# A 96-byte tile that nothing uses, opened first on the right side of SBUF

## The chip, the cores and the metric

The kernel runs as one program on one core of a Trainium2 chip. The core has five instruction streams that matter here: TensorE for matmuls (PE in the profile; its weight loads have a row of their own, PEld), VectorE (DVE), ScalarE (ACT), GpSimd (POOL) and SyncE (SP), which in this kernel issues every DMA. The metric is the device time of one execution in microseconds, taken as the median of several executions.

## The reference, cut to what matters

One layer of a hybrid streaming encoder in float32, for a prompt of 2048 tokens and a sample of 32 tokens with a cache of 128.

```python
qa, ka, va, qb, kb, vb = split_proj(rmsnorm(hp, g_attn[i]), w_in[i])   # 1024 -> 3072 columns
oa = diff_attn_prompt(qa, ka, va, t5_table, lam)     # group A: 4 heads, two score maps each, all earlier chunks
ob = band_attn_prompt(qb, kb, vb, band_table[i])     # group B: 8 heads, this chunk and the 8 before it
hp = hp + merge(oa, ob, subln_g[i], out_norm_b[i], w_out[i], lam_init)
c  = rmsnorm(h, g_mlp)
h  = h + jnp.square(jax.nn.relu(c @ w_up)) @ w_down                    # 1024 -> 4096 -> 1024
return h + jax.nn.sigmoid(h @ w_ple_gate) * (p @ w_ple_proj)
```

A last rmsnorm gives the outputs; the keys and values are outputs too. The sample goes through the same layer with its cache.

## The kernel before, in words

**Numbers as pairs.** A float32 product is made from two rounded parts. `split` writes the rounded part of a tile (`hi`, on ScalarE) and the rest (`lo`, a subtraction on GpSimd or VectorE). `mm3` then multiplies hi by hi, hi by lo and lo by hi (lines 216, 217 and 218) and adds the three in PSUM. In `mm3` the left member of a term is the stationary operand, which a weight load puts into the array, and the right member is the moving operand, which is read from SBUF column by column while the next weight load runs. In the profile a matmul is named out<-moving,stationary. In the products with weights the weight is stationary and the activation moves, except in the value projection `vps`, where the weight moves.

**Stages.** The 2080 tokens are four blocks, 512, 512, 512 and 544. Through the first 2050 us or so come the projections (`qps`, `vps`), both attentions (`s`, `sb`, `tpp`, `tpb`, `o`, `ob`), the output projection (`ops`) and the MLP of blocks 0 and 1 (`mlp`, with `ups` and `dps`). Then the gate of block 1 (`gps`, `pps`), the output projection of blocks 2 and 3, the gate of block 0, the MLP of block 2 (`mlp7`), the gate of block 2, the MLP of block 3 and its gate. `mlp7` makes the up projection with seven products of half size in place of eight, so its `ups` matmuls move 256 columns for block 2 and 272 for block 3, from the operand tiles `cs`. Its `dps` matmuls move the activations `uh` and `ul`, 512 columns for block 2 and twice 272 for block 3.

**Two sides of SBUF.** Each partition of SBUF is handed out from both ends. A pool opened with `side="left"` (the default) lies above the pools opened before it on the left; one with `side="right"` lies below those opened before it on the right. A tile takes a multiple of 32 bytes in each partition. A pool's place is thus the sum of the sizes of the pools that are open before it on its side. In the compiled program of the kernel before, the right side begins at byte 229,344, which is 32 past a multiple of 64. Where the right-side pools then lie:

| pool | opened for | tiles, bytes each | lowest byte | over a multiple of 64 |
|---|---|---|---|---|
| `pp0` | first blocks' inputs `x`, `xt` | 6 of 4096, 9 of 32 | 204,480 | 0 |
| `wv0` | first value weights `wh0`, `wl0` | 8 of 4096 | 171,712 | 0 |
| `a0`, `a1`, `b`, `wq` | attention, norms | `ka`, `e`, `pH`, `v`, `q` and others | 129,248 (`a1`) | 32 |
| `uh` | activations: `ou`, `hu`, `uh`, `ul`, `pT` | 20 of 2176 | 185,824 | 32 |
| `wx` | the fourth of each ring of weight pieces, `s2` | 5 of 2048 | 175,584 | 32 |
| `wk4` | temporaries and raw weights of the last stages | 2176 and 4096 | 136,928 | 32 |
| `fk4` | last norm: `gf` and small tiles | one of 4096, 21 pieces of 32 | 132,160 | 0 |
| `cs` | operands of `mlp7`; last gate's `hc` | 14 of 4352 | 71,232 | 0 |

The tiles of the left side that take part in matmuls (`aH`, `wh`, `wl`, `cH`, `hH`, the left pieces, and `uh` of the earlier MLP in pool `uq`) lie at multiples of 64. Columns within these tiles are taken in steps of 1024, 1088, 2048 or 2176 bytes, all multiples of 64, so a slice keeps its tile's remainder.

**Weights of the last stages.** From about 2120 us on `wunit` cuts each weight unit into two halves, and each half takes a hi and a lo piece from two rings whose turns go three times to the left (pool `wp4`) and once to the right (pool `wx`): `self.pieces = [Rings(*[(self.wp, t)] * 3, (wx, t)) for t in ("wh", "wl")]`. Every fourth piece is on the right.

**Order of the work.** Each engine runs one stream of instructions in an order fixed when the program is built, by a planner that sorts the work by priorities and by its own estimate of times. Buffers are handed out in rings: a tile waits for the last reader of the buffer that it takes over, also where the bytes belonged to a closed pool.

Of the kernel before, what the change touches and what calls it, by code (L numbers as in the profile page):

```python
# [13 lines left out]
F32 = mybir.dt.float32  # L14
# [6 lines left out]
P = 128  # L21
# [122 lines left out]
class Kern:  # L144
# [1311 lines left out]
    def run(self):  # L1456
        tc, nc, a = self.tc, self.nc, self.a
        with ExitStack() as top:

            def opened(stack, name, bufs, space=None, side="left"):  # L1460
                kw = {} if space is None else {"space": space}
                return stack.enter_context(
                    tc.tile_pool(name=name, bufs=bufs, side=side, reuse_waits="tile", **kw)
                )
# [4 lines left out]
            wpx = ExitStack()  # L1469
            self.wp = opened(wpx, "wp", 3)  # L1470
            self.rawp = Rings((self.wp, "wr"))
            mm = opened(top, "mm", MM, PSUM)
            tp = mm
            psx = ExitStack()
# [237 lines left out]
```

## Time and profile before

| | us |
|---|---|
| median of 3 runs | 3154.2 |
| lowest, highest | 3153.26, 3156.3 |
| profiled execution, its span from first to last instruction | 3144.6 |
| TensorE busy in the span | 3011.4 |
| VectorE, ScalarE, GpSimd busy | 1897.6, 1878.1, 1847.6 |

Of the profiled execution the page gives the span alone; the median of the runs is 9.6 us above it, which is the time around the span. The span is one execution's. A row of the page names a line, an engine, an operation and the tiles, and then tells the count, the time in sum and the mean of one in ns; a matmul's duration there is longer than the distance to the next one's start, since matmuls overlap. The timeline gives starts, and from a row of matmuls without a gap the time that one takes from the stream is (last start - first start) / count.

### The profile page before, as it was taken

Reading aid. Unit: us, or ns where it says so; the run is one execution under the profiler, and the core shown is the slowest. Engines: PE = TensorE matmul, PEld = TensorE weight load, DVE = VectorE, ACT = ScalarE, POOL = GpSimd, SP = SyncE. Lnnn points to the kernel's source line nnn. Section 1 sums busy time; section 2 is a strip of 40 time slices with the busy share of each in tenths; the row PEclk is TensorE's granted clock in tenths of the full one; section 3 lists DMA queues with packets and bytes.
Section 4 is the critical chain, followed back from the end, with each engine's and each line's share of the span. In section 5 each row is a group of like instructions: output and inputs, shape, how many; then the busy total and the mean of one; then the engine's idle time right before and its main releaser. Section 6 shows DMA issues by size and latency. Waiting matters only on the chain. (4 is left out here: it accounts for less than half of the span.)

```text
span 3144.6 us, 52811 instructions
## 1 busy us (share of the span) xinstructions
PE 3011.4 (96%) x17913; PEld 2649.6 (84%) x17913; DVE 1897.6 (60%) x4596; ACT 1878.1 (60%) x4166; POOL 1847.6 (59%) x2496
## 2 busy tenths in 40 slices
PE   8999898999999999999999999999899999999998
PEld 7787786899977887878788888878788887999998
DVE  5157774645465654666756556535667885576653
ACT  6257775766676764776666656554555455554545
POOL 2357455332345644665655545667877888667674
PEclk9999999999999999999999999999999999999999
DMA  8788757986788746555564543437533446333231
GB/s 281 244 244 244 204 185 229 263 232 201 205 250 230 218 130 153 152 154 153 157 184 130 144 123 103 145 116 241 179 128 115 144 152 229 123 107 107 88 116 56
DMA packets 523287, 539.27 MB, mean 171 GB/s; under 512 B 38749, under 2 KB 401569, under 8 KB 523017
## 3 DMA queue, kind: packets, MB, share of 16 engines
q1 hardware_dynamic: 523016, 535.89, 57.5%
q8 instruction: 142, 2.33, 0.3%
q14 instruction: 129, 1.05, 0.1%
HBM read 421.97 MB, written 117.75 MB: 172 GB/s over the span
## 5 line engine op out<-in xcount | busy, mean ns | idle before, releaser
L176 POOL TENSOR_TENSOR wl<-wr,wh 128x256 fp32r<-128x256 f32 x648 | 475.6, 766 | 354.8 <-ACT wh L181 315.7
L181 ACT ACTIVATE piece<-wr 128x512 fp32r<-128x512 f32 x406 | 246.1, 626 | 272.7 <-PE ups L217 113.1
L176 POOL TENSOR_TENSOR piece<-wr,piece 128x256 fp32r<-128x256 f32 x404 | 327.4, 837 | 99.7 <-ACT piece L181 86.4
L181 ACT ACTIVATE wh<-wr 128x1024 fp32r<-128x1024 f32 x228 | 241.2, 1058 | 171.7 <-PE qps L217 40.7
L166 POOL TENSOR_TENSOR wl<-wr,wh 128x256 fp32r<-128x256 f32 x264 | 199.4, 787 | 194.1 <-ACT wh L181 183.9
L216 PE MATMUL dps<-uh,piece 128*128 128x272 f32 (+1 forms) x768 | 247.0, 325 | 7.5 <-ACT piece L181 3.2
L166 POOL TENSOR_TENSOR piece<-wr,piece 128x256 fp32r<-128x256 f32 x280 | 237.0, 878 | 26.9 <-ACT piece L181 21.5
L218 PE MATMUL dps<-uh,piece 128*128 128x272 f32 (+1 forms) x768 | 247.8, 325 | 1.6 <-POOL piece L166 1.3
L217 PE MATMUL dps<-ul,piece 128*128 128x272 f32 (+1 forms) x768 | 247.8, 323 | 0.0
L216 PE MATMUL ups<-cs,piece 128*128 128x256 f32 (+1 forms) x864 | 246.0, 285 | 1.0 <-DVE r L1232 1.0
L217 PE MATMUL ups<-cs,piece 128*128 128x256 f32 (+1 forms) x864 | 245.3, 284 | 0.0
L218 PE MATMUL ups<-cs,piece 128*128 128x256 f32 (+1 forms) x864 | 245.2, 284 | 0.0
L216 PE MATMUL qps<-aH,wh 128*128 128x512 f32 (+1 forms) x640 | 231.2, 361 | 7.3 <-ACT kn L506 4.0
L218 PE MATMUL qps<-aH,wl 128*128 128x512 f32 (+1 forms) x640 | 229.5, 359 | 0.0
L217 PE MATMUL qps<-aL,wh 128*128 128x512 f32 (+1 forms) x640 | 228.5, 357 | 0.0
L1173 DVE TENSOR_TENSOR h<-h,dps 128x512 f32<-128x512 f32 x256 | 174.3, 683 | 80.9 <-PE dps L218 75.4
L1221 DVE TENSOR_TENSOR h<-h,dps 128x272 f32<-128x272 f32 (+1 forms) x384 | 189.3, 515 | 51.8 <-PE dps L218 50.8
L216 PE MATMUL dps<-uh,wh 128*128 128x512 f32 x512 | 207.8, 406 | 9.4 <-DVE h L1173 5.7
L216 PE MATMUL ups<-cH,wh 128*128 128x512 f32 x512 | 202.8, 396 | 2.1 <-ACT cH L181 1.1
L638 PE MATMUL s<-ka,q 128*128 128x512 f32 (+3 forms) x768 | 187.2, 345 | 15.9 <-ACT e L652 7.1
L218 PE MATMUL dps<-uh,wl 128*128 128x512 f32 x512 | 201.7, 394 | 0.5 <-POOL wl L166 0.4
L217 PE MATMUL ups<-cL,wh 128*128 128x512 f32 x512 | 201.2, 393 | 0.0
(317 smaller groups left out, 9634.2 us busy)
## 6 DMA issues: line engine op xcount, KB each, us to landing
wr<-w_up SPq DMA_DIRECT2D x128, 512.0 KB, 4.0
wr<-w_down SPq DMA_DIRECT2D x128, 512.0 KB, 3.8
wr<-w_in SPq DMA_DIRECT2D x74, 512.0 KB, 5.1
q<-qS SPq DMA_DIRECT2D x128, 256.0 KB, 5.4
v<-vSa SPq DMA_DIRECT2D x64, 512.0 KB, 3.9
ka<-kS SPq DMA_DIRECT2D x32, 512.0 KB, 8.9
wr<-w_out SPq DMA_DIRECT2D x32, 512.0 KB, 4.7
wr<-w_ple_gate SPq DMA_DIRECT2D x32, 512.0 KB, 4.3
```

Of the source, the lines that this page charges most:

```text
L166: nc.gpsimd.tensor_tensor(out[:, sl], a[:, sl], b[:, sl], op=op)
L176: nc.gpsimd.tensor_tensor(out[:, sl], a[:, sl], b[:, sl], op=op)
L181: nc.scalar.activation(hi, raw, AF.Copy)
L216: nc.tensor.matmul(ps, lh, rh, start=start and i == 0, stop=False)
L217: nc.tensor.matmul(ps, lh, rl, start=False, stop=False)
L218: nc.tensor.matmul(ps, ll, rh, start=False, stop=stop and i == n - 1)
L638: nc.tensor.matmul(s, q[:, m, hl, P * qi : P * qi + nr], kt[:, m, k0 - kb : k0 - kb + n], start=hl == 0, stop=hl == 1)
L1173: nc.vector.tensor_tensor(hv, hv, ps, op=ALU.add)
L1221: nc.vector.tensor_tensor(hv, hv, ps, op=ALU.add)
```

## The change

In `run`, right after the left pool for weights, a pool of one buffer is opened on the right side, before any other right-side pool of SBUF, and one tile of 24 float32 per partition (96 bytes) is taken from it. Nothing writes or reads the tile, and the pool stays open to the end of the kernel. Every other right-side tile lies 96 bytes lower than before. The words that go with the change say that all other right-side tiles then lie at multiples of 64 bytes.

```diff
             wpx = ExitStack()
             self.wp = opened(wpx, "wp", 3)
             self.rawp = Rings((self.wp, "wr"))
+            opened(top, "edge", 1, side="right").tile([P, 24], F32, name="edge")
             mm = opened(top, "mm", MM, PSUM)
```

## The prediction

> **What bounds the kernel now.** I read the page first: the span, the busy shares, the slices.
>
> ```profile
> span 3144.6 us, 52811 instructions
> PE 3011.4 (96%) x17913; PEld 2649.6 (84%) x17913; DVE 1897.6 (60%) x4596; ACT 1878.1 (60%) x4166; POOL 1847.6 (59%) x2496
> PE   8999898999999999999999999999899999999998
> PEclk9999999999999999999999999999999999999999
> ```
>
> TensorE is busy 3011.4 of 3144.6 us and in nearly every slice; no other engine passes 60%. The kernel ends when the stream of matmuls ends. A change of addresses can reach the time in two ways: it makes matmuls take less or more of the stream, or it moves a wait in the 133 us (3144.6 - 3011.4) in which TensorE stood idle. Next I read TensorE's waits and, by windows, the first stage and the two stages of the last MLPs.
>
> ```profile
> PE o L727 <- ACT pH L720: 7.8, 4, 3.7
> PE s L638 <- ACT e L652: 7.1, 9, 2.9
> PE xp L378 <- DMA x<-x_prompt: 5.4, 2, 4.5
> PE s L638 <- DMA q<-qS: 3.6, 4, 1.6
> PE sb L835 <- DMA q<-qS: 3.1, 1, 3.1
> ```
>
> ```profile
> core 0: us, PE busy (x) PEld busy (x) DVE busy (x) ACT busy (x) POOL busy (x), PEclk, DMA share, GB/s
> 0.00:60.00 60.00, 48.11 (x370) 45.10 (x371) 39.03 (x136) 43.57 (x132) 20.70 (x35) 1.00 0.98 303
> 2300.00:2640.00 340.00, 330.90 (x2026) 291.35 (x2025) 262.37 (x409) 178.12 (x355) 272.34 (x312) 1.00 0.46 150
> 2700.00:3066.00 366.00, 365.03 (x2912) 364.70 (x2911) 245.56 (x493) 185.31 (x338) 261.45 (x330) 1.00 0.34 108
> ```
>
> The waits are many small ones. In the last MLPs TensorE is idle 9.1 of 340 us and 1.0 of 366 us, so what a matmul there gains or loses goes to the end almost whole.
>
> **The change part by part.** The change adds no instruction, no DMA and no wait. The tile is neither written nor read. Its 96 bytes push every right-side tile down by 96, one and a half times 64, so each changes its remainder over 64: 32 becomes 0, and 0 becomes 32. By the table of pools this is not quite what the words of the change say. `uh`, `wx`, `wk4` and the attention pools go to multiples of 64; `cs`, `fk4`, `pp0` and `wv0`, which are there now, leave them. All right-side tiles move together, so which of them share bytes stays; against the closed left pools only the edges move by 96 bytes, onto tiles whose last reader is thousands of instructions back. I cost new waits at nothing: what covers them is that distance. I also expect the same order of instructions, since sizes and dependences stay; the chance that the planner sorts otherwise is kept as a case.
>
> So the question is whether any engine works at another rate at another remainder. The trace of before has both remainders side by side, on the left and on the right. First the three elementwise engines (groups by form, then GpSimd's medians from the views of lines 166 and 176; the columns there are min/median/max ns):
>
> ```profile
> L181 ACT ACTIVATE uh<-relu 128x512 fp32r<-128x512 f32 x64 | 40.5, 632 | 0.8
> L1237 ACT ACTIVATE r<-r 128x512 f32<-128x512 f32 x32 | 20.2, 633 | 1.0
> L1221 DVE TENSOR_TENSOR h<-h,dps 128x272 f32<-128x272 f32 x256 | 104.9, 433 | 45.5 <-PE dps L218 44.6
> L1232 DVE TENSOR_TENSOR r<-u,ups 128x272 f32<-128x272 f32 x32 | 13.8, 431 | 9.8 <-PE ups L218 8.6 <-POOL u L166 0.9
> L166 POOL TENSOR_TENSOR ul<-relu,uh x128: 728/740/1190, 1069.1 to 2045.5; 128x256 fp32r<-128x256 f32 x128
> L166 POOL TENSOR_TENSOR hu<-h,hu x8: 730/738/1238, 2637.5 to 2647.4; 128x256 fp32r<-128x256 f32 x8
> ```
>
> The first of each pair is on the left, the second on the right (of `hu<-h,hu` the `h` is left): 632 and 633, 433 and 431, 740 and 738 ns. I cost these engines at zero, between -2 and +2 ns of some 700; TensorE's work covers it, and if that cover were gone 2 ns on 2496 GpSimd instructions would be 5 us.
>
> TensorE is another matter. Here are its groups by form, then the timeline of three stretches without a gap.
>
> ```profile
> L216 PE MATMUL gps<-hu,piece 128*128 128x512 f32 x128 | 51.7, 404 | 8.0 <-ACT piece L181 6.5 <-DVE hd L980 1.5
> L216 PE MATMUL gps<-hH,wh 128*128 128x512 f32 x64 | 25.2, 393 | 0.0
> L216 PE MATMUL ops<-ou,piece 128*128 128x512 f32 x64 | 25.5, 399 | 0.4 <-ACT piece L181 0.4
> L216 PE MATMUL pps<-pT,piece 128*128 128x512 f32 x32 | 12.6, 395 | 0.0
> L216 PE MATMUL dps<-uh,piece 128*128 128x512 f32 x256 | 100.8, 399 | 7.5 <-ACT piece L181 3.2 <-ACT uh L181 2.5 <-DVE h L1221 1.8
> L216 PE MATMUL dps<-uh,piece 128*128 128x272 f32 x512 | 146.2, 288 | 0.0
> L216 PE MATMUL ups<-cs,piece 128*128 128x272 f32 x432 | 125.0, 289 | 1.0 <-DVE r L1232 1.0
> L216 PE MATMUL ups<-cs,piece 128*128 128x256 f32 x432 | 121.0, 281 | 0.0
> L216 PE MATMUL ups<-cs,lead 128*128 128x256 f32 x16 | 4.5, 280 | 0.0
> ```
>
> ```profile
> 2233.73 0.40 PE L216 MATMUL gps<-hu,piece 128*128 128x512 f32 x1
> ...
> 2236.53 0.39 PE L216 MATMUL gps<-hu,piece 128*128 128x512 f32 x1
> ...
> 2239.28 0.40 PE L216 MATMUL pps<-pT,piece 128*128 128x512 f32 x1
> ```
>
> ```profile
> 2078.61 0.39 PE L218 MATMUL gps<-hH,wl 128*128 128x512 f32 x1
> ...
> 2083.17 0.39 PE L217 MATMUL gps<-hL,wh 128*128 128x512 f32 x1
> ```
>
> ```profile
> 2399.88 0.40 PE L216 MATMUL dps<-uh,piece 128*128 128x512 f32 x1
> ...
> 2401.27 0.28 PE L216 MATMUL ups<-cs,piece 128*128 128x256 f32 x1
> ```
>
> The stretch from 2233.73 to 2239.28 is one group of 24. `hu` is on the right at remainder 32 throughout; by the ring's turns the first twelve take their weights from left pieces (remainder 0), the last twelve from right ones (32). The first twelve take 2.80 us, 233.3 ns each; the last twelve 2.75 us, 229.2 ns. With both on the left (`hH`, `wh`, both at 0) twenty take 4.56 us, 228.0 ns. So a 512-column matmul takes about 5.3 ns more where moving and stationary operand have different remainders, and almost none where they agree. I read that as the price of the mixed pair. After the change `hu`, `ou`, `pT`, `uh`, `ul` and all pieces lie at 0, and no pair of these is mixed. Three of four are mixed now, as three turns of four of the ring are left. With three rows (216, 217, 218) of each form:
>
> - `gps`: 3 x 128 x 3/4 = 288 matmuls, x 5.3 ns = 1.5 us.
> - `ops<-ou`: 3 x 64 x 3/4 = 144, 0.8 us.
> - `pps`: 3 x 32 x 3/4 = 72, 0.4 us.
> - `dps`, 512 columns: 3 x 256 x 3/4 = 576. Its six from 2399.88 to 2401.27 take 1.39 us, 231.7 ns, 3.7 above 228.0: 2.1 us. Between zero and 3.1 us (at 5.3 ns).
>
> That is a gain of 4.8 us. Against it stand the tiles that go to 32. `ups<-cs` has 3 x (432 + 16) = 1344 matmuls of 256 columns and as many of 272. They agree now in three of four and would be mixed in all. For 272 columns the trace has the mixed case: `dps<-uh,piece`, 288 ns, beside `ups<-cs,piece`, 289 ns. I take zero. For 256 columns it has none; the bounds are -1 ns (the difference of the 272-column rows) and 5.3 ns (the 512-column price), -1.3 to +7.1 us. I take 0.5 ns, 0.7 us, as the 272-column row is far nearer in length. The first stage's `vps` with weights from `wv0` is 8 token tiles x 2 halves x 24 = 384 of 256 columns; at 0.5 ns 0.2 us, at most 2.0, and that stage has 11.9 us of idle TensorE to take it. In attention both operands are right-side tiles and go together: nothing.
>
> DMAs keep their count and sizes. I cost a different landing time at nothing, as the few waits of TensorE for a DMA, above, are 1.6 to 4.5 us at the longest. If that cover goes, the `q` loads are late next.
>
> Sum: 3144.6 - 4.8 + 0.9 = 3140.7 us for the span; with the 9.6 us around it 3150.3. This is 0.12% under the median of 3154.2. A measurement of this kernel can tell about 0.2% (6.3 us, 3147.9 to 3160.5) from no change, so my forecast is no change by that bound.
>
> [...]
>
> **The rivals.**
>
> *Addresses do nothing.* The 4 ns between the two halves of that group could come from the side (left weights with right activations lie far apart) rather than from the remainder; the sides stay. For it: the 272-column rows show nothing. Against it: nothing in the trace, since side and remainder go together there. Time 3154.2, with the spread of the runs. [...]
>
> *Transfers into right-side tiles land sooner.* If a start at a multiple of 64 helps DMA writes, TensorE's waits for `q` (3.6 + 3.1 us) go, on top of the 3.9: 3154.2 - 3.9 - 6.7 = 3143.6, faster by 0.34%. For it: the first stages run the DMA engines near full (0.98 in the first 60 us). Against it: that stage's `x` goes the other way, to 32, and in the last MLPs the engines are less than half busy.
>
> *The operands of `mlp7` lose.* If a mixed pair costs the full 5.3 ns at 256 and at 272 columns, `ups<-cs` loses 2688 x 5.3 = 14.2 us, less the 4.8 gained: 3154.2 + 9.4 = 3163.6, slower by 0.30%. It decides from (6.3 + 4.8) / 2688 = 4.1 ns for each. Against it: 288 beside 289 ns, where the mixed form is the shorter.
>
> *The planner orders the work otherwise.* The tile could shift some tie in its estimates. Nothing in the profile prices that; I allow 10 us to either side.
>
> **How the numbers follow.** The mixed pairs, as summed: 0.46. Addresses do nothing: 0.25. Both end within 0.2%. Transfers land sooner: 0.15. The `mlp7` operands lose: 0.09. Another order: 0.05, of it 0.02 faster and 0.03 slower. So faster 0.17, same 0.71, slower 0.12. The likeliest case alone runs from 3145 (gains 1.5 + 0.8 + 0.4 + 3.1, losses at their lower end of -1.3, and 2 us of spread between runs) to 3161 (no gain in `dps`, 256 columns at 7.1, the same spread). For eight in ten I reach down to the faster rival and leave out the slower one: 3143 to 3161. The predicted time is 3150.3 us.
>
> **What would show it.** Right: the same counts of instructions in the same order, `gps<-hu,piece` with a mean like that of `gps<-hH` (393 ns, from 404), twelve matmuls of the first gate in 2.75 us whichever piece they take, `ups<-cs` of 256 columns still near 281. Wrong: `gps<-hu` still at 233 ns a matmul (the side, not the remainder), `ups<-cs` above 285 (the loss), a different order on any engine, or the idle time before `s` and `sb` gone (the transfers).

## The result and the profile after

The changed kernel takes 3146.46 us (median of 19 runs, 3131.61 to 3152.06). The kernel before, run beside it, takes 3150.71 us (19 runs, 3144.11 to 3156.3). The ratio is 0.9983, 95% interval [0.9975, 0.9991]: by the ratio 5.4 us less, 0.17% (the medians lie 4.3 us apart), which is within the 0.2% that the forecast took as no change, though the interval reaches past it. The granted clock does not explain it: over the 90 executions of before that have a clock on record, 0.001 of clock goes with 1.1 us, and the changed kernel's mean clock is 0.9843 beside their 0.9841. The forecast of 3150.3 us, with its range of 3143 to 3161, holds the time. Most of the forecast's reasons do not hold, as the experiments show.

The page of the changed kernel, the same lines as were shown of before:

```profile
span 3141.4 us, 52810 instructions
PE 3009.3 (96%) x17913; PEld 2651.0 (84%) x17913; DVE 1897.7 (60%) x4596; ACT 1876.7 (60%) x4166; POOL 1841.0 (59%) x2496
PE   8999898999999999999999999999899999999998
PEclk9999899999999999999999999999999999999999
```

The counts of matmuls and of elementwise work are the same, and the busy times agree within 2.1 us on TensorE, 1.4 on ScalarE, 6.6 on GpSimd. The order on each engine is the same. One instruction is gone, 52,810 in place of 52,811: before, the first `sqacc` of the pool `wq` overlapped the last 96 bytes under the end of a left-side buffer `xt` (137,184 + 2176 = 139,360, and `xt` begins at 139,264), so ScalarE waited there for the store of `xt`. Moved down by 96, the two only touch, and the wait is not built. In the trace of before that wait is passed in 17 ns while ScalarE works on something else, so it had no price.

The waits of TensorE (engine, tile and line, what it waited for, us in total, times, longest):

```profile
PE s L638 <- ACT e L652: 7.1, 9, 3.0
PE o L727 <- ACT pH L720: 6.0, 4, 2.7
PE xp L378 <- DMA x<-x_prompt: 4.6, 1, 4.6
PE s L638 <- DMA q<-qS: 3.5, 4, 1.8
PE sb L835 <- DMA q<-qS: 2.2, 1, 2.2
```

Each is within 1.8 us of its row before (7.1, 7.8, 5.4, 3.6, 3.1). No single wait went away. What about the matmuls that the forecast rested on? First the groups by form, then one gate group of 24 in the timeline, the one that took 2.80 and 2.75 us before:

```profile
L216 PE MATMUL gps<-hu,piece 128*128 128x512 f32 x128 | 51.8, 405 | 10.0 <-ACT piece L181 7.6 <-DVE hd L980 1.5 <-DVE tmp L1021 0.9
L216 PE MATMUL gps<-hH,wh 128*128 128x512 f32 x64 | 25.2, 393 | 0.0
L216 PE MATMUL ops<-ou,piece 128*128 128x512 f32 x64 | 25.6, 400 | 0.4 <-ACT piece L181 0.4
L216 PE MATMUL dps<-uh,piece 128*128 128x512 f32 x256 | 100.5, 398 | 6.7 <-DVE h L1221 2.5 <-ACT piece L181 2.3 <-ACT uh L181 1.8
L216 PE MATMUL ups<-cs,piece 128*128 128x272 f32 x432 | 124.6, 288 | 1.6 <-DVE r L1232 1.6
L216 PE MATMUL ups<-cs,piece 128*128 128x256 f32 x432 | 121.1, 281 | 0.0
```

```profile
2230.03 0.39 PE L216 MATMUL gps<-hu,piece 128*128 128x512 f32 x1
...
2232.80 0.39 PE L216 MATMUL gps<-hu,piece 128*128 128x512 f32 x1
...
2235.55 0.39 PE L216 MATMUL pps<-pT,piece 128*128 128x512 f32 x1
```

`gps<-hu` did not fall to 393 ns; it stands at 405 (404 before). The first twelve of the group take 2.77 us, 230.8 ns each, where they took 233.3; the last twelve 2.75 us, 229.2, as before. So the pair that was mixed gained 2.5 ns, half of the 5.3 that the forecast took. `ups<-cs` of 256 columns, which went from remainder 0 to 32, stands at a duration of 281 as before.

Half of the mechanism in that group is not yet an answer, since 1080 matmuls (288 + 144 + 72 + 576) by 2.5 ns would be 2.7 us. Two questions were left for runs: do the last stages bring any of the 5.4 us, and if not, what does?

### The profile page after: what moved, and what is told of

It reads as the page before. It is cut to its first block, busy times and chain, and to the rows that moved or that the text cites. A ratio compares the mean times of both kernels' runs of the same rounds, so it can differ in the third digit from the quotient of the medians.

```text
span 3141.4 us, 52810 instructions
## 1 busy us (share of the span) xinstructions
PE 3009.3 (96%) x17913; PEld 2651.0 (84%) x17913; DVE 1897.7 (60%) x4596; ACT 1876.7 (60%) x4166; POOL 1841.0 (59%) x2496
## 5 line engine op out<-in xcount | busy, mean ns | idle before, releaser
L217 PE MATMUL dps<-ul,wh 128*128 128x512 f32 x512 | 201.8, 394 | 0.0
```

What stands on the lines that cost most here:

```text
L217: nc.tensor.matmul(ps, lh, rl, start=False, stop=False)
```

## The experiments

All ratios are to the kernel before, run beside each, with their 95% intervals. Where a kernel leaves work out, its expectation says so.

### In which half of the kernel is the gain?

Three kernels were run together. `late` opens the unused tile only for the last stages, `early` only for those ahead of them, and `all64` adds two tiles of 32 bytes, so that the tiles which the change takes off a multiple of 64 (`x`, `wh0`, `gf`, `cs`, `hc`) are put back on one.

```diff
--- late
-            opened(top, "edge", 1, side="right").tile([P, 24], F32, name="edge")
...
+            opened(top, "edge", 1, side="right").tile([P, 24], F32, name="edge")
             up = Sized(opened(top, "uh", 20, side="right"), BLK)
```

> The same unused tile, but opened only right before the pool of the last MLPs' activations: first stages and attention as before, last stages as with the change. Mixed pairs (theory): -4.8 + 0.7 = -4.1 us against before, ratio 0.9987, so all that the change brings. By the 2 to 3 ns a matmul that the trace of after shows, 1080 x 2.5 = 2.7 less some 1 us for the operands of the seven products: -1.7 us, ratio 0.9995. Rival, the gain comes from the first 1250 us or so (transfers into right-side tiles, or attention's matmuls): ratio 1.000.

```diff
--- early
+            ex = ExitStack()
+            opened(ex, "edge", 1, side="right").tile([P, 24], F32, name="edge")
...
+            ex.close()
             up = Sized(opened(top, "uh", 20, side="right"), BLK)
```

> The same unused tile, open from the start but closed right before the pool of the last MLPs' activations: attention's tiles at multiples of 64, the first stage's inputs and value weights at 32, last stages as before. Mixed pairs (theory): +0.2 us for the value projection, ratio 1.0001. Rival, attention or transfers bring the gain: ratio 0.9983, all that the change brings. If both carry a part, this and the late tile add up to 0.9983.

```diff
--- all64 (beside the change)
             with ExitStack() as x:
+                opened(x, "edge0", 1, side="right").tile([P, 8], F32, name="edge0")
                 pp = opened(x, "pp0", 3, side="right")
...
+            opened(top, "edge4", 1, side="right").tile([P, 8], F32, name="edge4")
             fk = opened(top, "fk4", 1, side="right")
```

> The change, and a further unused 32-byte tile before the first stage's right-side pools and one before the pools of the last norm and of the seven products' operands: so all right-side tiles that matmuls read lie at multiples of 64. Mixed pairs (theory): no loss is left, 0.9 us less than with the change alone: ratio to before 0.9980 to 0.9985. Rival, remainders of the seven products' operands do not matter: as with the change, 0.9983. Rival, they lose in full: 2688 x 1 ns or more back, 0.9975 or less.

Measured: `late` 1.000 [0.999, 1.001], `early` 0.9975 [0.9966, 0.9984], `all64` 0.9978 [0.9968, 0.9988]. The forecast's place for the gain is wrong: with the last stages alone changed nothing comes that can be told from zero (the interval is 3 us wide to each side), and with the last stages as before all of it comes. `all64` cannot be told from the change.

A row on the first and last `ups` matmul is in line with this. The stretch between them holds both `mlp7`, one gate and nearly all `dps` matmuls of 512 columns. Rows of before, of after and of `late` (count, ns least/median/most, first start to last start):

```profile
L216 PE MATMUL ups<-cs,piece x864: 275/284/394, 2291.7 to 3049.1; 128*128 128x256 f32 x87, 128*128 128x272 f32 x86
```

```profile
L216 PE MATMUL ups<-cs,piece x864: 276/283/395, 2288.5 to 3046.3; 128*128 128x256 f32 x87, 128*128 128x272 f32 x86
```

```profile
L216 PE MATMUL ups<-cs,piece x864: 276/283/392, 2300.5 to 3057.8; 128*128 128x256 f32 x87, 128*128 128x272 f32 x86
```

The stretch takes 757.4 us before, 757.8 after and 757.3 in `late`. Its remainders changed and its length did not by more than single executions differ: over all twelve kernels traced here it takes 755.1 to 760.2 us. The change begins it 3.2 us earlier. That alone says little, as `late`, whose addresses up to there are those of before, begins it 8.8 us later.

### What do mixed pairs cost by themselves?

`probe` runs rows of 72 matmuls of one form, with the operands at chosen starts:

```diff
+            for w, m, s, side in CASES if rep == "busy" else CASES[::-1]:
+                for j in range(N):
...
+                    nc.tensor.matmul(
+                        o[:, :w],
+                        st[side[1]][:, s // 4 + 128 * (j % 8) : s // 4 + 128 * (j % 8) + 128],
+                        mov[side[0]][:, m // 4 + 544 * (j % 3) : m // 4 + 544 * (j % 3) + w],
```

> Leaves the whole computation out: it writes zeros and runs only rows of 72 matmuls of one form back to back, once beside running ScalarE, VectorE, GpSimd and DMA work and once with those engines idle. Moving and stationary operand start 0, 4, 16, 32 or 48 bytes past a multiple of 64, on the left, on the right, or the moving one right and the stationary one left. Mixed pairs (theory): at 512 columns (0,0) and (32,32) take about 228 ns from start to start, (0,32) and (32,0) about 233, on either side; at 256 and 272 columns mixed and equal pairs agree within 1 ns. Rival, the moving operand's own remainder: (32,0) and (32,32) both 2 to 5 ns above (0,0) and (0,32). Rival, the side: left-left 228, right-left 233, whatever the remainders. Rival, neither: every form within 1 ns of 228, in both passes; then what the trace of before showed hangs on the other engines' traffic or on the kernel's own stream.

Rows with the other engines idle. In a name, `m32s0rl` is: moving operand 32 past a multiple of 64 and on the right, stationary one at a multiple and on the left.

```profile
L80 PE MATMUL w512m0s0rlidle<-mr,sl x72: 387/392/397, 551.9 to 568.3; 128*128 128x512 f32 x72
L80 PE MATMUL w512m32s0rlidle<-mr,sl x72: 392/396/398, 535.1 to 551.7; 128*128 128x512 f32 x72
L80 PE MATMUL w512m32s32rlidle<-mr,sl x72: 388/392/397, 501.7 to 518.1; 128*128 128x512 f32 x72
L80 PE MATMUL w512m0s0llidle<-ml,sl x72: 392/395/398, 702.9 to 719.4; 128*128 128x512 f32 x72
L80 PE MATMUL w512m32s0llidle<-ml,sl x72: 389/395/398, 686.1 to 702.6; 128*128 128x512 f32 x72
```

From the first start to the last are 71 matmuls. With the moving operand right and the stationary one left, equal remainders take 16.35 us, 230.3 ns each (0 with 0; 32 with 32 takes 230.4), and the mixed pair 16.56 us, 233.3. With both on the left the mixed pair and the pair at 0 take the same 16.57 us (the pair at 32 takes 16.43), and with both on the right all four pairs take 16.55 to 16.57. The right-left rows of the other pass, beside running engines, say the same (230.5 and 233.2 ns). So there is an effect of 3.0 ns in one arrangement and none to be relied on in the others. The forecast's 5.3 ns as a price of every mixed pair falls. 228 ns is reached by no row of the idle pass.

The arrangement with an effect is the one that the kernel has, so the kernels' own matmuls can be priced. The operands' places are in the compiled programs, and the traces give the distance from each start to the next; distances of 215 to 250 ns are taken, so that waits do not count. Of the forecast's 1080 matmuls with 512 columns and a left piece, some 1025 are left. They take 232.9 ns on the mean before and 232.8 in `early`, where they are mixed, and 231.1 after and 231.0 in `late`, where they are not. The 350 with a right piece take 231.2 before and 231.4 after. The price of a mixed pair is thus 1.8 ns, and the term 1.9 us in place of 4.8. The `ups<-cs` matmuls with left pieces (distances of 100 to 140 ns, some 1010 of each width), which the change makes mixed, go from 117.6 to 118.6 ns at 256 columns and from 125.8 to 125.2 at 272. Together this is a gain of 1.5 us in the last stages, too little for `late` to show.

### Which tiles of the first part, and is it the remainder over 64?

`bonly` moves the pool of the second attention (and `wq`, which lies on it), `aonly` the two pools of the first attention. `e64` keeps the tile open throughout with 64 bytes: everything moves, no remainder over 64 changes.

```diff
--- bonly
+            opened(bx, "edge", 1, side="right").tile([P, 24], F32, name="edge")
             bp = opened(bx, "b", 1, side="right")
--- aonly (the same ahead of a1)
+                opened(x, "edgea0", 1, side="right").tile([P, 24], F32, name="edgea0")
                 pool = opened(x, "a0", 1, side="right")
--- e64
-            opened(top, "edge", 1, side="right").tile([P, 24], F32, name="edge")
+            opened(top, "edge", 1, side="right").tile([P, 16], F32, name="edge")
```

> The unused tile opened right before the second attention's pool and closed with it, from about 500 to 1230 us: only that pool and the norm's that lies on it move to multiples of 64. New theory, transfers: this pool holds the loads with the small runs (vbt in runs of 512 bytes, kbt, bb), so it brings most of what the early tile brought: ratio 0.998 to 0.9985. Rival, the first attention (its pools a0 and a1): 1.000. Rival, each carries its part: 0.9988.

> The unused tile opened right before each of the two pools of the first attention and closed with it: only these tiles move to multiples of 64. New theory, transfers into the second attention's pool: 0.9995 to 1.000. Rival, the first attention: 0.9975 to 0.998. Rival, each carries its part: 0.9988.

> The unused tile with 64 bytes in place of 96, from start to end: every right-side tile moves down, none changes its remainder over 64. Theory that the remainder decides: 1.000. Rival, the shift as such (which tiles share bytes with closed left pools, or a coarser boundary) decides: 0.998.

Measured: `bonly` 0.9996 [0.9987, 1.0006], `aonly` 0.9999 [0.9988, 1.0011], `e64` 1.0004 [0.9995, 1.0012]. A shift that keeps the remainders brings nothing. But neither part alone shows a gain either. So four more were run together, on another chip: `early` once more (`early2`), all three attention pools (`ab`, the edits of `aonly` and `bonly` in one), the pool `setup` alone, and `e32`, with 32 bytes, which gives every tile the same remainder over 64 as the change.

```diff
--- setup
+                opened(x, "edge", 1, side="right").tile([P, 24], F32, name="edge")
                 wk = opened(x, "setup", 1, side="right")
--- e32
-            opened(top, "edge", 1, side="right").tile([P, 24], F32, name="edge")
+            opened(top, "edge", 1, side="right").tile([P, 8], F32, name="edge")
```

> The early tile once more (open from the start, closed before the last MLPs' activations), beside the next three on one chip. Theory that the tiles of the first 1450 us carry the gain: 0.9966 to 0.9984 again. Rival, its first value was a matter of that chip and hour: 0.999 to 1.000, as the parts gave.

> The unused tile before all three attention pools (a0, b, a1), closed with each: all of attention at multiples of 64, the first stage's inputs and the setup pool as before. Theory that attention's tiles carry the gain together (each part too small to tell from zero alone): like the early tile, 0.998. Rival, the parts add up as measured, -0.04% and -0.01%: 0.9995. Rival, the setup pool is the missing part: 0.9995, and the next run 0.998.

> The unused tile before the pool of the biases and of the inputs of the last gate (setup) alone, closed with it. Theory that attention carries the gain: 1.000. Rival, this pool (the only one beside attention's that the early tile and the kernel with two further tiles both move by half of 64): 0.998.

> The unused tile with 32 bytes in place of 96, from start to end: the same remainders over 64 as with the change, another shift. Theory that remainders decide: as the change, 0.9975 to 0.9991, and as the early tile within 0.001. Rival, the shift or a coarser boundary (96 is no multiple of 128 either, but other tiles cross 128): 1.000.

Measured: `early2` 0.9994 [0.9985, 1.0003], `ab` 0.9987 [0.9977, 0.9997], `setup` 1.0004 [0.9995, 1.0014], `e32` 1.0002 [0.9993, 1.0011]. Two things come out of this.

First, the same kernel gave 0.9975 on one chip and 0.9994 on another, and the two intervals do not meet. By 1.1 us for 0.001 the granted clock covers some 1.4 of the 6.0 us between them (`early` 0.9850 beside 0.9843 for before, `early2` 0.9836 beside 0.9841). An interval of one comparison holds for that chip and hour; the size of the gain is known only as somewhere between 0 and 0.25%.

Second, `e32` has the remainders over 64 that the change has, and has no gain. So 64 bytes are not the boundary of the gain. Before, the attention pools begin 96 past a multiple of 128. Moved by 96 they begin at a multiple of 128 (of `v`, `pH` and `pL` half the buffers go from 32 past one to 64 past one), and the second attention's tiles `vbt` at a multiple of 256 (183,904 - 96 = 183,808 = 718 x 256). Moved by 32 or 64 they do not. Sorted by that, and with two columns from the profiles:

| kernel | attention's pools over a multiple of 128 | ratio | store of `t`, 136 KB, us | first `ups<-cs,piece`, us |
|---|---|---|---|---|
| before | 96 | 1 | 4.3 | 2291.7 |
| `late` | 96 | 1.000 | 4.6 | 2300.5 |
| `setup` | 96 | 1.0004 | 4.4 | 2300.2 |
| `e32` | 64 | 1.0002 | 4.5 | 2296.4 |
| `e64` | 32 | 1.0004 | 4.6 | 2295.3 |
| `aonly` | first at 0, second at 96 | 0.9999 | 4.2 | 2291.7 |
| `bonly` | first at 96, second at 0 | 0.9996 | 3.9 | 2301.3 |
| `ab` | 0 | 0.9987 | 3.9 | 2291.7 |
| `early2` | 0 | 0.9994 | 3.9 | 2291.5 |
| the change | 0 | 0.9983 | 3.6 | 2288.5 |
| `all64` | 0 | 0.9978 | 3.8 | 2293.9 |
| `early` | 0 | 0.9975 | 3.8 | 2288.2 |

The five kernels with all of attention at a multiple of 128 have a mean ratio of 0.9983, and each lies below each of the four with none of it there (mean 1.0003). They begin `mlp7` at 2290.8 us on the mean, the five traces with none there (before among them) at 2296.8. Each trace is one execution, and the two groups overlap by 2 us (2293.9 and 2291.7), so the 6.0 us are rough; from that matmul to the end of the span both groups take 853 us, so what is gained is gained before it.

Two landmarks split the stretch before it: the last `ob` matmul, with which the second attention ends, and the last `o` matmul, with which the first does. Here are their rows in `aonly`, then in `bonly`:

```profile
L887 PE MATMUL ob<-pb,vbt x352: 191/392/774, 524.9 to 1201.2; 128*128 128x512 f32 x120, 128*128 128x256 f32 x48, 128*128 128x64 f32 x8
...
L729 PE MATMUL o<-pH,v x296: 258/282/420, 202.0 to 2008.7; 128*128 128x256 f32 x144, 128*128 128x32 f32 x4
```

```profile
L887 PE MATMUL ob<-pb,vbt x352: 192/392/792, 524.4 to 1207.5; 128*128 128x512 f32 x120, 128*128 128x256 f32 x48, 128*128 128x64 f32 x8
...
L729 PE MATMUL o<-pH,v x296: 257/282/416, 199.2 to 2018.3; 128*128 128x256 f32 x144, 128*128 128x32 f32 x4
```

Up to the last `ob` the five lead by 3.7 us (1200.2 and 1204.0 on the mean), and from there to the last `o` by 2.6 more (807.8 and 810.4). In this second stretch `aonly`, whose first attention has moved, takes 807.5 us, and `bonly`, whose first attention has not, 810.8. So a part of the gain goes with the first attention's tiles, after the second attention has ended.

### What do the transfers do?

The views of DMA issues, from 100 to 1450 us, hold packets, MB and busy share of the queue, and the median us from issue to landing. Before, after, `e32` and `bonly`, in this order:

```profile
q1 hardware_dynamic: 276363, 275.99, 71.4%
...
oT<-t SPq DMA_DIRECT2D x8, 136.0 KB, 4.3
```

```profile
q1 hardware_dynamic: 277106, 278.09, 70.7%
...
oT<-t SPq DMA_DIRECT2D x8, 136.0 KB, 3.6
```

```profile
q1 hardware_dynamic: 276291, 276.13, 71.0%
...
oT<-t SPq DMA_DIRECT2D x8, 136.0 KB, 4.5
```

```profile
q1 hardware_dynamic: 275851, 275.12, 70.0%
...
oT<-t SPq DMA_DIRECT2D x8, 136.0 KB, 3.9
```

After, the queue moves 0.8% more in the window and is busy a smaller share of it: 70.7 / 278.09 against 71.4 / 275.99 is 1.7% less time per MB; `bonly` has 1.7% less too, `e32` 0.6%. This share alone does not decide: `e64`, without a gain, has 70.6% for 276.78 MB, 1.4% less. The stores of `t` from the second attention's pool land in 3.6 to 3.9 us in all six kernels where that pool is at a multiple of 128, and in 4.2 to 4.6 in all others. Packet by packet, the 512-byte packets of the queue while the 576 KB loads of `vbt` (runs of 512 bytes) were under way take a mean of 29.2 to 30.4 ns in these six and 31.8 to 32.5 in the others. On the mean that is 29.7 beside 32.1 ns, the same data in some 7.5% less time. Why a packet takes longer at the other starts, no run shows. The first attention shows the same: from 1230 to 2020 us the queue's 4096-byte packets, loads of `ka` among them, take 301.6 to 304.5 ns in the six kernels whose first attention is at a multiple of 128 and 310.6 to 318.3 in the others. There `ka` lies 128 past a multiple of 256, so a boundary of 256 alone does not cover it.

That loads do not see 32 bytes by themselves is what `dmaprobe` says, with 24 DMAs of a form in a row and nothing else running (the end of a name is the pass, a or b):

```diff
+                    t = right.tile([P, 1216], F32, tag="in", name=f"in{b}r{r}{rep}")
...
+                        nc.sync.dma_start(
+                            t[:, r // 4 : r // 4 + 1024].rearrange("p (k c) -> p k c", k=n),
```

> Leaves the whole computation out: it writes zeros, and moves the input into right-side tiles and one tile out again, 24 DMAs of one form in a row, TensorE idle. Forms: runs of 512, 1024, 2048, 4096 and 4736 bytes in a partition (stores: 512, 1024, 2176), the tile's start 0 or 32 bytes past a multiple of 64, in two passes of opposite order. New theory, transfers into right-side tiles land sooner at a multiple of 64: per packet some 5 to 8% less at remainder 0, as in the trace (loads of vbt: 29.9 ns a packet of 512 bytes after, 32.3 before; 4736 bytes 292 after, 310 before). Rival, DMA does not see the remainder: equal within 1% in both passes.

```profile
in4736r32b<-x_prompt SPq DMA_DIRECT2D x24, 592.0 KB, 12.0
in4736r0b<-x_prompt SPq DMA_DIRECT2D x24, 592.0 KB, 12.0
...
in512r32b<-x_prompt SPq DMA_DIRECT2D x24, 512.0 KB, 7.3
in512r0b<-x_prompt SPq DMA_DIRECT2D x24, 512.0 KB, 7.3
...
out2176r0a<-o SPq DMA_DIRECT2D x24, 272.0 KB, 6.3
out2176r32a<-o SPq DMA_DIRECT2D x24, 272.0 KB, 6.7
out2176r32b<-o SPq DMA_DIRECT2D x24, 272.0 KB, 5.8
out2176r0b<-o SPq DMA_DIRECT2D x24, 272.0 KB, 6.2
```

No form of load gains from remainder 0 in both passes (512 bytes in the first pass: 7.2 us at 0 and 6.3 at 32). But the loads' tiles lay 64 past a multiple of 128, so their two starts were 64 and 96, and the coarser boundary was not among them. They tell against 64 bytes, as `e32` does, and leave 128 and 256 untried. The tile of the stores began at a multiple of 128, so their starts were 0 and 32 past one. Runs of 2176 bytes, which the stores of `t` have too, landed 0.4 us sooner at 0 in one pass and 0.4 us later in the other. With nothing else running, a start at a multiple of 128 thus shows no gain for such stores.

## Why the prediction was right in number and wrong in reason

- **The base of the sum.** "The 9.6 us around it" is an error. Single executions have both numbers: the profiled one of the changed kernel took 3143.18 us with a span of 3141.4, so 1.8 us lie around the span. The other 7.8 us came from setting a quick execution of before against a median of slower ones. The step happened to do no harm, since only differences count. But before itself took 3150.71 us beside the change, 3.5 less than its first three runs, so 3150.3 is nearly the time of no change at all.
- **The same work in the same order.** Right. That the change adds no wait was right too; it takes one away, worth 17 ns.
- **Elementwise engines, zero.** Right: DVE 1897.7 us for 1897.6, ACT 1876.7 for 1878.1; POOL is 6.6 us lower, under cover.
- **A mixed pair costs 5.3 ns, 4.8 us in sum.** This term failed by its size. There is a price, but over all such matmuls it is 1.8 ns, 1.9 us in sum; the group that gave the 5.3 gained 2.5 ns, and the separate rows give 3.0 ns in one arrangement and none in another. A term of 5 ns was read from twelve matmuls, beside twenty of another stage, and multiplied by 1080. The start-to-start distance of one form varies by more than the price with nothing mixed: the probe's equal pairs take 230.3 ns in one arrangement and 233.3 in another.
- **Losses of `ups<-cs` and `vps`, 0.9 us.** Small, as said: 1.0 ns more for the matmuls of 256 columns, 1.0 us in sum, and none for those of 272 (0.6 ns less). The losing rival (14.2 us on `ups<-cs`) is excluded by the 757.8 us. `vps` was not priced by itself.
- **"In attention both operands are right-side tiles and go together: nothing", and "I cost a different landing time at nothing".** These are the steps that missed the gain. Most of the 5.4 us lies ahead of 2290 us and goes with attention's tiles; only some 1.5 us are the forecast's. The first sentence is not quite right either, as the transposes `tpp` and `tpb` take `ident` from the left, but they start 109 ns apart before and after. That the forecast's gain of 3.9 us and the measured one are close is luck: one term was more than twice too large, and a gain of about that size was not in the sum.
- **The table of remainders over 64.** The forecast took the boundary from the words of the change and never looked at 128 or 256. `e32` and `e64` show that 64 decides nothing that the time tells from zero.
- **The rivals.** "Addresses do nothing" is within 3 us what the last stages show (`late` 1.000), though the 1.8 ns of the kernels' matmuls and the 3.0 of the probe do not fit it to the letter. "Transfers into right-side tiles land sooner" comes nearest to the rest: landings did shorten in attention (the stores of `t` from 4.3 to 3.6 us), though at a coarser boundary and without removing the `q` waits that it named (3.5 and 2.2 us remain of 3.6 and 3.1). For the first stage nothing is shown: `x` lands in 5.5 us after and in 6.4 before, but in 6.7 in `early`, where it lies as after.

What is shown: the gain is gone when attention's tiles stay, or move by 32 or 64, and it is there, in varying size, when they all move by 96 (four of the five intervals end below 1, that of `early2` does not). What is only argued: that shorter packets are its cause. Against that stand `bonly`, which has the shorter packets of the second attention and a ratio of 0.9996, and the stores of `dmaprobe`; for it, that the interval of `bonly` reaches 0.9987 and that the packets of each attention shorten where its own tiles have moved. The cause stays open. A kernel with `vbt` and `t` alone at a multiple of 256, and a probe of loads with starts 0 and 128, were not tried. The grouping by 128 was made after the runs, so it has not been put to a test of its own. No version beats the change by more than its interval.

## What to carry to other kernels

Take a price per instruction from many groups, not from one, before it is multiplied by a thousand, and look whether the stretch that holds them changes length. A change of addresses moves every tile's place with regard to all powers of two at once: vary the shift (32, 64, 96) before naming the boundary. When a gain is near 0.2%, repeat the same kernel on another chip, as its size may not repeat (0.9975 and 0.9994 here).

## What was not expected of the hardware

- Start-to-start distances of a 512-column matmul lie between 229.2 and 233.3 ns for equal work, by arrangement; a remainder of 32 between a moving operand on the right and a stationary one on the left explains 1.8 ns of it in the kernels and 3.0 in the probe, and none in the probe's other arrangements.
- Stores of `t` with 136 KB land in 3.6 to 3.9 us when their pool begins at a multiple of 128 bytes and in 4.2 to 4.6 when it does not, 64 past such a multiple included. In `dmaprobe`, with nothing else running, stores with the same run length show no such difference.
- The same program's ratio to the same reference was 0.9975 on one chip and 0.9994 on another.
